# Split-GELU gate, fp32: loads on ScalarE's queue, stores on SyncE's, GELU in place, redundant waits dropped

## Chip, cores, metric

One core of one Trainium2 chip. The metric is the device time of one execution in microseconds (us). The kernel before took 470.53 us (median of 3 runs, 470.52 to 470.63). "Faster" or "slower" here start at 2%.

## The reference

```python
def setup_inputs():
    batch, seq, dim = (32, 512, 2048)
    return {'x': np.random.randn(batch, seq, dim).astype(np.float32)}

def reference(x):
    half_dim = x.shape[-1] // 2
    x1, x2 = x[..., :half_dim], x[..., half_dim:]
    gelu_x1 = 0.5 * x1 * (1 + erf(x1 / np.sqrt(2)))
    return (gelu_x1 * x2).astype(np.float32)
```

134.22 MB are read, 67.11 MB written, and per output element there is one GELU and one multiply.

## The kernel before

16 tiles of 128 partitions x 8 rows x 2048 columns; two x tiles and two o tiles. A load is 8.39 MB, a store 4.19 MB. The first and the last tile are cut into pieces.

```python
R = 8
xpool = tile_pool(name="xpool", bufs=2)
opool = tile_pool(name="opool", bufs=1)
o_tiles = [opool.tile([P, R, half], ...) for k in range(2)]

def load(i):
    x_tile = xpool.tile([P, R, dim], ...)
    for rows in (slice(0, 4), slice(4, 8)) if i == 0 else (slice(0, 8),):
        dma = nc.sync.dma_start(out=x_tile[:, rows, :], in_=x_t[i][:, rows, :])
        before_gelu[i % 2].append(dma.ins)
    return x_tile
# ... store(queue, i, o_tile, rows): the same for a store
ahead = [load(0), load(1)]
for i in range(n_tiles):
    # ... steps: row ranges of a tile, (0,5),(5,8) in the middle tiles
    for lo, hi in steps:
        nc.scalar.activation(out=o_tile[:, rows, :], in_=x_tile[:, rows, :half], func=GELU)
        mul = nc.vector.tensor_mul(out=o_tile[:, rows, :], in0=o_tile[:, rows, :],
                                   in1=x_tile[:, rows, half:])
        for ins in before_gelu[i % 2]:
            tc.declare_no_dep(mul.ins, ins, reason="ScalarE waited for it")
        # ... pieces: store on nc.sync if last, else on nc.scalar
    if not pieces:
        store(nc.sync if i == n_tiles - 2 else nc.scalar, i, o_tile, slice(0, R))
    if i + 2 < n_tiles:
        ahead.append(load(i + 2))
```

GELU writes into the o tile, so it has to wait for the store that still reads that o tile.

Of the kernel before, what the change touches and what calls it, by code (L numbers as in the profile page):

```python
# [1 line left out]

# [4 lines left out]

GELU = mybir.ActivationFunctionType.Gelu


@with_exitstack
def kernel(
    ctx: ExitStack,
    tc: tile.TileContext,
    x: bass.AP,
    out: bass.AP,
):











    nc = tc.nc
    P = nc.NUM_PARTITIONS  # L30

    x_flat = x.flatten_outer_dims()
    out_flat = out.flatten_outer_dims()
    n_rows, dim = x_flat.shape
    half = dim // 2

    R = 8
    x_t = x_flat.rearrange("(n p r) d -> n p r d", p=P, r=R)
    o_t = out_flat.rearrange("(n p r) d -> n p r d", p=P, r=R)
    n_tiles = x_t.shape[0]  # L40

    xpool = ctx.enter_context(tc.tile_pool(name="xpool", bufs=2))
    opool = ctx.enter_context(tc.tile_pool(name="opool", bufs=1))
    o_tiles = [opool.tile([P, R, half], out.dtype, name=f"o{k}_tile") for k in range(2)]

    def load(i):
        x_tile = xpool.tile([P, R, dim], x.dtype, name="x_tile")
        for rows in (slice(0, 4), slice(4, 8)) if i == 0 else (slice(0, 8),):
            dma = nc.sync.dma_start(out=x_tile[:, rows, :], in_=x_t[i][:, rows, :])  # L49
            before_gelu[i % 2].append(dma.ins)  # L50
        return x_tile

    def store(queue, i, o_tile, rows):
        dma = queue.dma_start(out=o_t[i][:, rows, :], in_=o_tile[:, rows, :])
        before_gelu[i % 2].append(dma.ins)


    before_gelu = [], []

    ahead = [load(0), load(1)]  # L60
    for i in range(n_tiles):
        x_tile = ahead.pop(0)
        o_tile = o_tiles[i % 2]
        last = i == n_tiles - 1
        pieces = i == 0 or last
        steps = ((0, 2), (2, 4), (4, 8)) if pieces else ((0, 5), (5, 8))
        muls = []
        for lo, hi in steps:
            rows = slice(lo, hi)
            tc.keep_in_program_order(  # L70
                nc.scalar.activation(  # L71
                    out=o_tile[:, rows, :], in_=x_tile[:, rows, :half], func=GELU
                )
            )
            mul = nc.vector.tensor_mul(  # L75
                out=o_tile[:, rows, :],
                in0=o_tile[:, rows, :],
                in1=x_tile[:, rows, half:],
            )
            for ins in before_gelu[i % 2]:  # L80
                tc.declare_no_dep(mul.ins, ins, reason="ScalarE waited for it")
            muls.append(mul.ins)
            if pieces and hi % 4 == 0:
                store(nc.sync if last else nc.scalar, i, o_tile, slice(hi - 4, hi))
        before_gelu[i % 2].extend(muls)
        if not pieces:
            store(nc.sync if i == n_tiles - 2 else nc.scalar, i, o_tile, slice(0, R))
        if i + 2 < n_tiles:
            ahead.append(load(i + 2))


# [1 line left out]
_INS = ['x']  # L93
_OUTS = [((32, 512, 1024), 'float32')]


# [23 lines left out]
```

## Time and profile before

A queue here is the list of DMAs that one engine issues. A DMA lands when the engines that wait for it see that all its bytes have arrived. The DMA share is the mean busy share of the core's 16 DMA engines.

| | before |
|---|---|
| time, median | 470.53 us |
| span of the profile (first to last instruction of the program) | 469.1 us |
| VectorE, ScalarE busy | 30%, 25% |
| DMA share, 1.7 to 467.9 us | 1.00 |
| bytes over the span | 429 GB/s |

The prediction below shows the lines that carry this. Two more views are needed. The first is the groups of instructions of the kernel before, different shapes apart (line, engine, operation, output<-inputs, shapes, count | busy us, mean ns of one | idle before, and what ended it; DVE is VectorE, ACT ScalarE, SP SyncE, and a q behind a name marks DMA issues):

```profile
L75 DVE TENSOR_TENSOR o_tile<-o_tile,x_tile 128x5120 f32<-128x5120 f32 x14 | 76.9, 5492 | 279.9 <-ACT o_tile L71 279.9
L71 ACT ACTIVATE o_tile<-x_tile 128x5120 f32<-128x5120 f32 x14 | 62.6, 4469 | 301.2 <-DMA out_dram<-o_tile 280.3 <-DMA x_tile<-in_x_dram 20.9
```

The last column shows ScalarE waiting for stores (`out_dram<-o_tile`) in nearly all its idle time. The second is the start of the timeline:

```profile
0.72 1.28 ACT L71 ACT_TABLE_LOAD   x1 [0.72 <-PEq L104]
0.73 403.84 SPq L49 DMA_DIRECT2D x_tile<-in_x_dram  x17
```

ScalarE loads its activation table while SyncE issues the first load.

### The profile page before, as it was taken

The numbers are of one execution on the slowest core, as the hardware profiler recorded it, in microseconds if no ns is written. First come the engines' busy times: TensorE is split into PE (matmuls) and PEld (weight loads), VectorE is DVE, ScalarE is ACT, GpSimd is POOL, SyncE is SP. The second block draws the span as 40 slices with busy tenths as digits, with TensorE's granted clock in tenths as the row PEclk, the third lists the DMA queues.
The fourth block names the chain that finished last, engine by engine and source line by source line (L and its number), as shares of the span: only waits on it lengthen the run. The fifth ranks groups of instructions, "written<-read, shape, count | busy, mean of one in ns | idle before, by whom it ended". The sixth has DMA issues, their size and how long they took to land.

```text
span 469.1 us, 179 instructions
## 1 busy us (share of the span) xinstructions
DVE 140.5 (30%) x34; ACT 115.5 (25%) x35; POOL 0.2 (0%) x4
## 2 busy tenths in 40 slices
DVE  0330615206051160611506015070250702407042
ACT  1320606041060410605005050050601406014060
POOL 0000000000000000000000000000000000000000
DMA  8999999999999999999999999999999999999998
GB/s 358 447 447 447 414 391 492 402 402 447 492 402 402 447 469 425 402 441 408 492 402 425 425 492 402 402 447 486 408 402 444 455 441 402 441 408 486 408 406 355
DMA packets 5041, 201.34 MB, mean 429 GB/s; under 512 B 560, under 2 KB 560, under 8 KB 560
## 3 DMA queue, kind: packets, MB, share of 16 engines
q1 hardware_dynamic: 2880, 142.61, 70.4%
q10 hardware_dynamic: 2160, 58.72, 29.0%
q14 instruction: 1, 0.01, 0.0%
HBM read 134.22 MB, written 67.11 MB: 429 GB/s over the span
## 4 chain that ended last, share of the span: by engine, by line
DMA 75%; DVE 14%; ACT 8%; ACTq 0%; issue 0%; SPq 0%
DMA out_dram<-o_tile 66%; DVE o_tile L75 14%; DMA x_tile<-in_x_dram 10%; ACT o_tile L71 8%; ACTq L115 0%; SPq L49 0%
## 5 line engine op out<-in xcount | busy, mean ns | idle before, releaser
L75 DVE TENSOR_TENSOR o_tile<-o_tile,x_tile 128x5120 f32<-128x5120 f32 (+3 forms) x34 | 140.5, 4171 | 320.4 <-ACT o_tile L71 320.4
L71 ACT ACTIVATE o_tile<-x_tile 128x5120 f32<-128x5120 f32 (+3 forms) x34 | 114.3, 3407 | 340.1 <-DMA out_dram<-o_tile 302.4
L71 ACT ACT_TABLE_LOAD x1 | 1.3, 1283 | 0.7 <-PEq L104 0.7
L104 POOL MEMSET const-bfloat16-1.0<- 128x1 bf16 x1 | 0.1, 101 | 0.0
L104 POOL MEMSET const-uint8-127<- 128x1 uint8 x1 | 0.1, 101 | 0.0
L104 POOL MEMSET const-float32-0.0<- 128x1 f32 x1 | 0.1, 98 | 0.2 <-issue 0.2
L104 POOL MEMSET const-float32-1.0<- 128x1 f32 x1 | 0.1, 98 | 0.0
## 6 DMA issues: line engine op xcount, KB each, us to landing
out_dram<-o_tile ACTq DMA_DIRECT2D x13, 4096.0 KB, 44.8
x_tile<-in_x_dram SPq DMA_DIRECT2D x2, 4096.0 KB, 16.8
out_dram<-o_tile ACTq DMA_DIRECT2D x2, 2048.0 KB, 34.3
out_dram<-o_tile SPq DMA_DIRECT2D x1, 4096.0 KB, 25.2
out_dram<-o_tile SPq DMA_DIRECT2D x2, 2048.0 KB, 7.5
x_tile<-in_x_dram SPq DMA_DIRECT2D x15, 44.6
```

The lines of the kernel that those rows point to most:

```text
L71: nc.scalar.activation(out=o_tile[:, rows, :], in_=x_tile[:, rows, :half], func=GELU)
L75: mul = nc.vector.tensor_mul(out=o_tile[:, rows, :], in0=o_tile[:, rows, :], in1=x_tile[:, rows, half:],)
L104: nc = _bacc.Bacc("TRN2", target_bir_lowering=False, num_devices=1)
```

## The change

The intent: each queue gets one direction; ScalarE no longer waits for a store before GELU (it writes x's own half); waits that another wait implies are declared away. `x_users` and `o_users` list the earlier instructions on the same x and o tile.

```diff
-    xpool = ctx.enter_context(tc.tile_pool(name="xpool", bufs=2))
+    xpool = ctx.enter_context(tc.tile_pool(name="xpool", bufs=1))
+    x_tiles = [xpool.tile([P, R, dim], x.dtype, name=f"x{k}_tile") for k in range(2)]
+    def no_wait(ins, others):
+        for other in others:
+            tc.declare_no_dep(ins, other, reason="implied by another wait")
...
-            dma = nc.sync.dma_start(out=x_tile[:, rows, :], in_=x_t[i][:, rows, :])
+            dma = nc.scalar.dma_start(out=x_tile[:, rows, :], in_=x_t[i][:, rows, :])
...
                 nc.scalar.activation(
-                    out=o_tile[:, rows, :], in_=x_tile[:, rows, :half], func=GELU
+                    out=x_tile[:, rows, :half], in_=x_tile[:, rows, :half], func=GELU
                 )
...
+            no_wait(gelu.ins, x_users[i % 2])
...
             mul = nc.vector.tensor_mul(
                 out=o_tile[:, rows, :],
-                in0=o_tile[:, rows, :],
+                in0=x_tile[:, rows, :half],
                 in1=x_tile[:, rows, half:],
             )
-            for ins in before_gelu[i % 2]:
-                tc.declare_no_dep(mul.ins, ins, reason="ScalarE waited for it")
+            no_wait(mul.ins, loads[i] + x_users[i % 2] + o_users[i % 2])
...
-            store(nc.sync if i == n_tiles - 2 else nc.scalar, i, o_tile, slice(0, R))
+            nc.sync.dma_start(out=o_t[i], in_=o_tile)
...
```

More of the change, by code (lines that the diff above doesn't have):

```diff
@@ L40 @@
     n_tiles = x_t.shape[0]
-    xpool = ctx.enter_context(tc.tile_pool(name="xpool", bufs=2))
+    xpool = ctx.enter_context(tc.tile_pool(name="xpool", bufs=1))
     opool = ctx.enter_context(tc.tile_pool(name="opool", bufs=1))
+    x_tiles = [xpool.tile([P, R, dim], x.dtype, name=f"x{k}_tile") for k in range(2)]
     o_tiles = [opool.tile([P, R, half], out.dtype, name=f"o{k}_tile") for k in range(2)]
+    def no_wait(ins, others):
+        for other in others:
+            tc.declare_no_dep(ins, other, reason="implied by another wait")
+    x_users, o_users = ([], []), ([], [])
+    loads = {}
     def load(i):
-        x_tile = xpool.tile([P, R, dim], x.dtype, name="x_tile")
+        x_tile = x_tiles[i % 2]
+        loads[i] = []
         for rows in (slice(0, 4), slice(4, 8)) if i == 0 else (slice(0, 8),):
-            dma = nc.sync.dma_start(out=x_tile[:, rows, :], in_=x_t[i][:, rows, :])
-            before_gelu[i % 2].append(dma.ins)
-        return x_tile
-    def store(queue, i, o_tile, rows):
-        dma = queue.dma_start(out=o_t[i][:, rows, :], in_=o_tile[:, rows, :])
-        before_gelu[i % 2].append(dma.ins)
-    before_gelu = [], []
-    ahead = [load(0), load(1)]
+            dma = nc.scalar.dma_start(out=x_tile[:, rows, :], in_=x_t[i][:, rows, :])
+            loads[i].append(dma.ins)
+    load(0)
+    load(1)
     for i in range(n_tiles):
-        x_tile = ahead.pop(0)
-        o_tile = o_tiles[i % 2]
+        x_tile, o_tile = x_tiles[i % 2], o_tiles[i % 2]
         last = i == n_tiles - 1
@@ L66 @@
         steps = ((0, 2), (2, 4), (4, 8)) if pieces else ((0, 5), (5, 8))
-        muls = []
+        gelus, muls = [], []
         for lo, hi in steps:
             rows = slice(lo, hi)
-            tc.keep_in_program_order(
+            gelu = tc.keep_in_program_order(
                 nc.scalar.activation(
-                    out=o_tile[:, rows, :], in_=x_tile[:, rows, :half], func=GELU
+                    out=x_tile[:, rows, :half], in_=x_tile[:, rows, :half], func=GELU
                 )
             )
+            no_wait(gelu.ins, x_users[i % 2])
             mul = nc.vector.tensor_mul(
                 out=o_tile[:, rows, :],
-                in0=o_tile[:, rows, :],
+                in0=x_tile[:, rows, :half],
                 in1=x_tile[:, rows, half:],
             )
-            for ins in before_gelu[i % 2]:
-                tc.declare_no_dep(mul.ins, ins, reason="ScalarE waited for it")
+            no_wait(mul.ins, loads[i] + x_users[i % 2] + o_users[i % 2])
+            gelus.append(gelu.ins)
             muls.append(mul.ins)
             if pieces and hi % 4 == 0:
-                store(nc.sync if last else nc.scalar, i, o_tile, slice(hi - 4, hi))
-        before_gelu[i % 2].extend(muls)
+                part = slice(hi - 4, hi)
+                nc.sync.dma_start(out=o_t[i][:, part, :], in_=o_tile[:, part, :])
         if not pieces:
-            store(nc.sync if i == n_tiles - 2 else nc.scalar, i, o_tile, slice(0, R))
+            nc.sync.dma_start(out=o_t[i], in_=o_tile)
+        x_users[i % 2].extend(gelus + muls + loads[i])
+        o_users[i % 2].extend(muls)
         if i + 2 < n_tiles:
-            ahead.append(load(i + 2))
+            load(i + 2)
 _INS = ['x']
```

## The prediction

> **What bounds the kernel now.** I read the page's busy shares first, then its DMA lines, then the busy time by stretch, and only then the waits.
>
> ```profile
> DVE 140.5 (30%) x34; ACT 115.5 (25%) x35; POOL 0.2 (0%) x4
> ...
> DMA  8999999999999999999999999999999999999998
> ...
> q1 hardware_dynamic: 2880, 142.61, 70.4%
> q10 hardware_dynamic: 2160, 58.72, 29.0%
> ...
> HBM read 134.22 MB, written 67.11 MB: 429 GB/s over the span
> ```
>
> VectorE and ScalarE are idle for 70% and 75% of the span. The 16 DMA engines show 90% or more in every slice but the first and the last, and their two queues' packets add up to 70.4 + 29.0 = 99.4% of the span. Both queues move bytes equally fast: 70.4% of 16 x 469.1 us is 5284 us for 142.61 MB, so 27.0 GB/s per engine; 29.0% is 2177 us for 58.72 MB, also 27.0 GB/s. So neither the queue nor the direction matters to the rate; bytes do.
>
> Where is the missing 0.6%? The stretches say it (columns: stretch, its length, busy time of VectorE, ScalarE and GpSimd, clock, DMA share, GB/s).
>
> ```profile
> 0.00:1.70 1.70, 0.00 (x0) 0.98 (x1) 0.20 (x4) 1.00 0.00 0
> 1.70:467.90 466.20, 140.48 (x34) 114.56 (x35) 0.00 (x0) 1.00 1.00 432
> ```
>
> From 1.70 to 467.90 us the DMA share is 1.00. The span has 1.7 us before the first packet (start barrier, then a load issued at 0.73 us, whose packets follow about 1.0 us later) and 1.2 us after the last one (landing of the store, the closing barrier). The floor of this program is therefore 201.33 MB at 432 GB/s = 466.0 us, plus 1.7, plus 1.2: 468.9 us, against a span of 469.1. The kernel stands within 0.1% of what its bytes allow.
>
> The waits look as if they contradict this:
>
> ```profile
> DVE o_tile L75 <- ACT o_tile L71: 320.4, 18, 20.9
> ACT o_tile L71 <- DMA out_dram<-o_tile: 302.4, 14, 22.0
> ACT o_tile L71 <- DMA x_tile<-in_x_dram: 37.8, 3, 20.9
> ```
>
> ScalarE waits 302.4 us for stores, which is just the wait that the change removes. But these are idle times of engines that do not set the end. What one tile in the middle does, and how long its transfers take to land:
>
> ```profile
> 100.48 7.12 ACT L71 ACTIVATE o_tile<-x_tile 128x5120 f32<-128x5120 f32 x2 [21.78 <-DMA out_dram<-o_tile]
> 104.98 8.76 DVE L75 TENSOR_TENSOR o_tile<-o_tile,x_tile 128x5120 f32<-128x5120 f32 x2 [20.14 <-ACT o_tile L71]
> 113.77 0.36 ACTq L54 DMA_DIRECT2D out_dram<-o_tile  x1
> ...
> out_dram<-o_tile ACTq DMA_DIRECT2D x1, 4096.0 KB, 44.7
> x_tile<-in_x_dram SPq DMA_DIRECT2D x1, 44.5
> ```
>
> The last two lines are the store and the load issued at 113.77 us: the load lands at 158.3 us, the store at 158.5. GELU starts at 158.49, on the later of the two.
>
> **What the Trainium skill says.** "DMA: Bandwidth & Descriptors", section "Issuing engines are not separate DMA queues": transfers from SyncE and ScalarE run on the same 16 DMA engines and interleave; using several issuers saves only issue time. This trace agrees: equal rates on both queues, worked out above. The same page, "Where 436 GB/s comes from", puts the ceiling of the path at 435 GB/s; the 432 here, over the whole stretch, leaves nothing to win in rate. "ScalarE: Activation LUTs", "What ACT_TABLE_LOAD costs", gives about 1283 ns for the load of the activation table and 186 ns + 0.833 ns per element for an ACTIVATE without pointer operands: 4451 ns for 5120 elements. The trace has 1.28 us and 4469 ns. "VectorE: DVE Perf Modes", the tier table, has fp32 tensor_tensor of 2048 elements at 2293 ns; the trace has 2288. The formula has no term for where the output lies, so in-place GELU should cost the same.
>
> **The change, part by part.**
>
> Queues swapped. No bytes, shapes or counts change: 17 loads and 18 stores before and after. A load issue takes 0.33 us on SyncE and a store issue 0.36 us on ScalarE; these sit inside the 15 us of slack worked out below, except the first. ScalarE passes the start barrier at the same moment as SyncE (its table load starts at 0.72 us, SyncE's first issue at 0.73). Here is a choice: does ScalarE load its table before or after it issues loads? A table load belongs to the first GELU, and the code issues loads 0 and 1 before it, so I expect it after the three issues, at about 2 us, long before GELU needs it at 12.9 us. Cost then 0.0. If it comes first, the first load issues 1.28 us later and the whole run ends 1.3 us later, since the DMA is never idle afterwards. I give that 20%.
>
> In the loop the new load stands in ScalarE's order behind the two GELUs of its tile and waits for VectorE's last multiply of that tile, so it is issued where it is now (113.77 us). ScalarE's next work is the GELU of the next tile, whose load lands some 15 us later, so this blocks nothing. SyncE now holds only stores, in order. The 2:1 ratio of bytes per load and per store is unchanged, and both queues stay filled.
>
> GELU in place. It writes x's own half and no longer waits for the store of two tiles ago; the multiply takes over that wait. Now GELU may start when the load lands, 0.2 us (158.3 against 158.5) before the store. The multiply starts at the later of (load landing + 4.48 us of first GELU) and the store's landing: 4.3 us after the store, not 4.5. The gain is 0.2 us of latency per tile, and that lies in slack: when the pair lands at about 100.4 us, the next load and store (8.39 + 4.19 MB, issued at 84.87 us) are still wholly outstanding, 29.0 us of DMA work at 434 GB/s, while the next issues come 13.3 us later. The reserve is 15.7 us per tile; making it 15.9 buys nothing.
>
> Dropped waits. Each is at most a 17 ns semaphore instruction of an idle sequencer; 0.0 us.
>
> The end. Load 15 lands at 448.8 us and the last compute starts at 449.17. The store issued at 433.30 lands 25.2 us later, 458.5, and covers the DMA until then. The first half of the last tile is stored from 455.6, the second from 460.9; the first is 2.10 MB, so it keeps the DMA busy until about 463, while the second's packets are ready about 1 us after its issue, 461.9. There is about 1 us to spare, and the change starts this chain up to 0.4 us earlier. Nothing won, nothing lost. Sum: 0.0 us, and 0.2 x 1.3 = 0.3 us on average for the table load.
>
> **The rivals.**
>
> The removed wait was real, and a faster chain pays: the chain of waits on the page goes through stores, GELU and multiply, with 7.8% for GELU and 14% for the multiply; if all first-GELU waits vanished, 14 x 4.5 = 63 us. Against it: the DMA share of 1.00 from 1.70 to 467.90 us. No chain can end before its bytes have moved, so the best case is 468.9 of span, about 0.2 us better.
>
> Loads on ScalarE's queue are held up behind a GELU. If a load were ordered after the next tile's GELU, it would be issued when that tile's load has landed plus 7.1 us of GELU and 1 us to the first packet; meanwhile only 4.19 MB of store (9.7 us) is outstanding. Even that barely fits; with another few us of delay there would be gaps of 1 to 3 us on each of 14 tiles, 480 to 510 us. For it: ScalarE is in order and now carries both. Against it: today's stores stand at the very same place of ScalarE's order and leave within 30 ns of the multiply's end.
>
> The table load goes first: +1.3 us, as above.
>
> **Range and chances.** The mean of the cases is 470.53 + 0.3, of which I keep little because it is one chance in five: 470.6 us. Downward there is only 0.2 us of span plus scatter (the three runs spread 0.1 us[...]). Upward there is 1.3 us. So 469.8 to 472.0 us eight times in ten. Faster by 2% would need 461.1 us, below the 466.0 us of the bytes alone: 0.5%. Slower by 2% needs 9.4 us of idle DMA, which only the second rival gives: 1.5%.
>
> **What would show it right or wrong.** Right: DMA slices stay at 9 throughout, the bytes change sides (about 134 MB on the queue that ScalarE feeds, 67 on SyncE's), ScalarE's waits name the loads and no store, the ACTIVATE and TENSOR_TENSOR durations stay at 4469 and 5492 ns, and VectorE still mostly waits for ScalarE. The table load's place is seen in the first row of ScalarE. Wrong: DMA shares below 1.00 in the middle, loads that issue well after the multiply's end, a multiply slowed by its strided first operand, or loads and stores on swapped queues that no longer land together, so that the last store begins later.

## The result, and the profile after

471.46 us median (471.11 to 471.99, 6 runs) against 470.53 us (470.46 to 470.73, 6 runs). The ratio is 1.002, 95% interval 1.0007 to 1.0033. Ratios here are the mean time of one kernel's fast runs over that of the other's of the same rounds, so not quite the ratio of the medians. So: the same within 2%, and slower by 0.2% beyond noise.

From the page of the changed kernel, the DMA slices and the queues (packets, MB, share of 16 engines' span):

```profile
DMA  8999999999999999999999999999999999999998
...
q10 hardware_dynamic: 2448, 134.22, 66.3%
q1 hardware_dynamic: 2592, 67.11, 33.2%
```

The bytes have changed sides as intended, 134 MB and 67 MB, and the DMA is as full as before. By stretch (columns as in the prediction):

```profile
0.00:1.70 1.70, 0.00 (x0) 0.00 (x0) 0.20 (x4) 1.00 0.00 0
1.70:467.90 466.20, 140.48 (x34) 115.54 (x35) 0.00 (x0) 1.00 1.00 432
```

The same 1.00 and 432 GB/s; the only difference is ScalarE's 0.98 us in the first 1.7 us, which is the table load that has moved. The waits of the changed kernel (who <- for whom: us in total, times, longest):

```profile
ACT x_tile L72 <- DMA x_tile<-in_x_dram: 338.4, 17, 21.9
DVE o_tile L77 <- ACT x_tile L72: 320.0, 18, 21.4
```

The 302.4 us for stores are gone from ScalarE, and it waits 338.4 us for loads: 302.4 + 37.8 = 340.2 before. A wait changed its name and kept its length. One tile in the middle, from the timeline:

```profile
100.79 7.12 ACT L72 ACTIVATE x_tile<-x_tile 128x5120 f32<-128x5120 f32 x2 [21.88 <-DMA x_tile<-in_x_dram]
105.29 8.76 DVE L77 TENSOR_TENSOR o_tile<-x_tile 128x5120 f32<-128x5120 f32 x2 [20.25 <-ACT x_tile L72]
114.08 0.36 ACTq L58 DMA_DIRECT2D x_tile<-in_x_dram  x1
```

The load leaves ScalarE 0.03 us after the multiply's end (105.29 + 8.76 = 114.05), so sharing an engine with GELU delays nothing. The groups, shapes apart:

```profile
L77 DVE TENSOR_TENSOR o_tile<-x_tile 128x5120 f32<-128x5120 f32 x14 | 76.9, 5492 | 279.7 <-ACT x_tile L72 279.7
L72 ACT ACTIVATE x_tile<-x_tile 128x5120 f32<-128x5120 f32 x14 | 62.6, 4469 | 301.0 <-DMA x_tile<-in_x_dram 301.0
```

5492 and 4469 ns, to the nanosecond those of before: GELU in place and a multiply with a strided first operand cost the same. The start of ScalarE's timeline, and the last stores, which SyncE issues:

```profile
0.74 1.35 ACTq L58 DMA_DIRECT2D x_tile<-in_x_dram  x3
2.11 1.28 ACT L72 ACT_TABLE_LOAD   x1 [2.11 <-issue]
...
455.31 5.57 SPq L87 DMA_DIRECT2D out_dram<-o_tile  x2
```

The three loads are issued first (0.74 us against 0.73), the table follows. The last tile's stores go out at 455.31 us and 5.2 us later, 0.3 us earlier than before, and it helps nothing.

Both profiles have a span of 469.1 us. The 0.9 us must then be outside the span, or in the scatter between runs: each run of the changed kernel has its own span, 468.7 to 469.6, and time minus span (the time of a run less its own span) is 2.29 to 2.41 us in all six. In the profiled run of before it was 470.87 - 469.1 = 1.8. That became the open question of the experiments, next to the claim that the compute chain has a reserve.

### The profile page after: what moved, and what is told of

The parts are those of the page before. It is cut to its first block, busy times and chain, and to the rows that moved or that the text cites. A ratio compares the mean times of both kernels' runs of the same rounds, so it can differ in the third digit from the quotient of the medians.

```text
span 469.1 us, 178 instructions
## 1 busy us (share of the span) xinstructions
DVE 140.5 (30%) x34; ACT 115.5 (25%) x35; POOL 0.2 (0%) x4
## 4 chain that ended last, share of the span: by engine, by line
DMA 75%; DVE 14%; ACT 8%; ACTq 1%; issue 0%
DMA x_tile<-in_x_dram 75%; DVE o_tile L77 14%; ACT x_tile L72 8%; ACTq L119 0%; ACTq L58 0%
## 5 line engine op out<-in xcount | busy, mean ns | idle before, releaser
L77 DVE TENSOR_TENSOR o_tile<-x_tile 128x5120 f32<-128x5120 f32 (+3 forms) x34 | 140.5, 4171 | 320.0 <-ACT x_tile L72 320.0
L72 ACT ACTIVATE x_tile<-x_tile 128x5120 f32<-128x5120 f32 (+3 forms) x34 | 114.3, 3407 | 338.4 <-DMA x_tile<-in_x_dram 338.4
```

The source lines that it names most:

```text
L72: nc.scalar.activation(out=x_tile[:, rows, :half], in_=x_tile[:, rows, :half], func=GELU)
L77: mul = nc.vector.tensor_mul(out=o_tile[:, rows, :], in0=x_tile[:, rows, :half], in1=x_tile[:, rows, half:],)
```

## The experiments

Twelve kernels, in three calls, each call on one chip with runs of the kernel before. "Before" took 470.63, 470.63 and 470.56 us (medians).

**1. The changed kernel again.** No edit.

> The changed kernel once more, to see whether its 0.9 us (ratio 1.002) repeat. Both profiles so far have a span of 469.1 us and the same DMA busy time, so the 0.9 us should again lie outside the span: time minus span 2.3 to 2.4 us. If they are scatter of one chip, the ratio is 1.000 here.

Measured: 471.31 us (471.03 to 471.58, 5 runs), before 470.63; ratio 1.0013 (1.0001 to 1.0026). Mean span 468.92 against 468.88 of before; mean time minus span 2.35 against 1.78. So of the 0.62 us between the mean times, 0.57 lie outside the span and 0.04 in it. The difference repeats and is not in the part where the kernel's work is.

**2. Queues only.** Before, with

```diff
-            dma = nc.sync.dma_start(out=x_tile[:, rows, :], in_=x_t[i][:, rows, :])
+            dma = nc.scalar.dma_start(out=x_tile[:, rows, :], in_=x_t[i][:, rows, :])
...
-                store(nc.sync if last else nc.scalar, i, o_tile, slice(hi - 4, hi))
+                store(nc.sync, i, o_tile, slice(hi - 4, hi))
...
-            store(nc.sync if i == n_tiles - 2 else nc.scalar, i, o_tile, slice(0, R))
+            store(nc.sync, i, o_tile, slice(0, R))
```

> Only the queues swapped, GELU still into o_tile with its old waits. If the swap of queues costs the 0.9 us (ScalarE's queue for loads), the ratio is 1.002. If the extra time is an instruction fetch after the end that depends on how many instructions each engine has, VectorE has as few here as before, and the ratio should be 1.000. In either theory the DMA share from 1.7 to 467.9 us stays 1.00 and the span 469.1.

Measured: 470.62 us, ratio 1.000 (0.9988 to 1.0013); span 468.88, time minus span 1.78. The swap of queues is worth nothing and costs nothing.

**3. In place and dropped waits only.** The changed kernel, with

```diff
-            dma = nc.scalar.dma_start(out=x_tile[:, rows, :], in_=x_t[i][:, rows, :])
+            dma = nc.sync.dma_start(out=x_tile[:, rows, :], in_=x_t[i][:, rows, :])
...
-                nc.sync.dma_start(out=o_t[i][:, part, :], in_=o_tile[:, part, :])
+                (nc.sync if last else nc.scalar).dma_start(out=o_t[i][:, part, :], in_=o_tile[:, part, :])
-            nc.sync.dma_start(out=o_t[i], in_=o_tile)
+            (nc.sync if i == n_tiles - 2 else nc.scalar).dma_start(out=o_t[i], in_=o_tile)
```

> GELU in place and the waits dropped, queues as before. If the dropped waits and in-place GELU were worth anything, it would show here undisturbed: the prediction says 0.0 us, ratio 1.000 (the rival of a shorter chain: 0.87 at its best). If the new waits of VectorE lengthen the end by an instruction fetch, ratio 1.002; if the swap of queues does it, 1.000.

Measured: 471.07 us, ratio 1.0011 (0.9999 to 1.0024); mean span 469.14, time minus span 2.04. The freed wait of ScalarE brings nothing here either. Outside the span there is half of the extra time, between the two theories as I had put them: neither named 2.04.

**4. Redundant waits left in.** The changed kernel, with

```diff
-        for other in others:
-            tc.declare_no_dep(ins, other, reason="implied by another wait")
+        return
```

> The changed kernel with every redundant wait left in (VectorE then waits for up to four semaphores per multiply). Prediction: the dropped waits are worth 0.0 us, so within 0.3 us of the changed kernel. If waits cost the DMA anything, the span grows over 469.1; if only the number of instructions per engine matters to the fetch at the end, the span stays and time minus span differs from the changed kernel's 2.4.

Measured: 470.94 us, ratio 1.0006 (0.9993 to 1.002); span 469.08, time minus span 1.86. The kernel with 30 more wait instructions on VectorE is not slower than the changed one (470.94 against 471.31): the dropped waits are worth 0.0 us in the span, and outside it their absence goes with a longer time.

**5. to 7. Padding the instruction streams.** Tiny instructions at the start, where the engine idles anyway: 14 GELUs on ScalarE of the changed kernel; 30 multiplies on its VectorE; 14 multiplies on VectorE of the kernel before. Shown for 5; 6 and 7 have their own count, take the multiply and put the tile in `opool`.

```diff
     load(1)
+    pad = xpool.tile([P, 4], x.dtype, name="pad")
+    nc.gpsimd.memset(pad, 0.0)
+    for _ in range(14):
+        nc.scalar.activation(out=pad, in_=pad, func=GELU)   # or: nc.vector.tensor_mul(out=pad, in0=pad, in1=pad)
```

> The changed kernel with 14 tiny GELUs (128x4) on ScalarE at the start, where it waits 9 us for the first load anyway, and one small memset on GpSimd. ScalarE then has 74 instructions instead of 60 (the queues-only kernel had 74 and its time minus span was 1.78 us). If the 0.6 us outside the span hangs on how many instructions the engines' streams hold, time minus span moves away from 2.35, most likely to 1.8, the span stays 468.9 to 469.2, and the kernel is as fast as before (ratio 1.000). If it comes from the change itself (queues with in-place GELU), it stays at 2.35, ratio 1.0013.

> The changed kernel with 30 tiny multiplies (128x4) on VectorE at the start: 86 instructions instead of 56, as many as the kernel with all waits kept, whose time minus span was 1.86 us. Stream length theory: time minus span about 1.9, span unchanged at 469.0, ratio about 1.0006. If it was the waits themselves that shortened that kernel's time, time minus span stays 2.35.

> The kernel before with 14 tiny multiplies on VectorE at the start: 56 instructions as in the changed kernel, with nothing else changed. Stream length theory: time minus span leaves 1.78 us, up to some 0.6 us, with the span unchanged at 468.9; that would make the kernel before slower by 0.1% with no part of the change in it. If the time outside the span belongs to the change, it stays 1.78 and the ratio 1.000.

Measured: 471.13 us (ratio 1.001, 0.9998 to 1.0023), 471.02 us (1.0009, 0.9996 to 1.0021) and 470.90 us (1.0007, 0.9993 to 1.002). The ratios alone say little. Span and time minus span say more, since the latter scatters by only some 0.05 us around its mean within a kernel (most in experiment 1: 2.22 to 2.41). Instructions are counted in the built programs; the kernels 9 to 12 are described below and stand here because they test the same thing:

| kernel | instructions ScalarE, VectorE | mean span | mean time minus span |
|---|---|---|---|
| before (call 1, call 2) | 72, 42 | 468.88, 468.87 | 1.78, 1.77 |
| queues only (2) | 74, 42 | 468.88 | 1.78 |
| before + 14 multiplies (7) | 72, 56 | 468.90 | 2.03 |
| in place only (3) | 69, 56 | 469.14 | 2.04 |
| changed + 14 GELUs (5) | 74, 56 | 469.06 | 2.06 |
| changed + 1 GELU (8, below) | 61, 56 | 469.20 | 2.05 |
| changed (1) | 60, 56 | 468.92 | 2.35 |
| changed + 30 multiplies (6) | 60, 86 | 469.16 | 1.89 |
| changed, waits kept (4) | 60, 86 | 469.08 | 1.86 |
| before (call 3) | 72, 42 | 468.80 | 1.79 |
| hardly any compute (9) | 39, 44 | 469.75 | 1.77 |
| multiplies twice (10) | 73, 84 | 469.77 | 1.76 |
| multiplies three times (11) | 73, 112 | 508.02 | 1.77 |
| late loads (12) | 61, 56 | 475.55 | 2.05 |

Experiment 7 is the clean one: nothing of the change is in it, the span does not move (468.90), and the time outside grows by 0.26 us. With 42 or 44 instructions on VectorE it is 1.77 to 1.79, with 56 it is 2.03 to 2.06, with 84 or more again 1.76 to 1.89. With 56 on VectorE, ScalarE at 60 goes with a further 0.3 us (2.35), at 61 or more it does not. So the time outside the span goes with the lengths of the instruction streams (the instructions of one engine, in order), up and down, and not with a queue, a wait or in-place GELU as such. The padded kernels also carry one memset on GpSimd and one instruction more on SyncE; experiment 12 has neither, and at 61 and 56 it too has 2.05. Of the three numbers that I had expected for 5 to 7, only that of 6 was met (1.89 for 1.9); 5 gave 2.06 and not 1.8, 7 gave part of its "up to 0.6". Why a certain length costs 0.3 us is open: the trace records nothing of the engines after the span. A fetch of instructions was my guess. The traces of the changed kernel have a packet of the instruction queue at 471.2 to 471.3 us, after the span, where the kernel before has one at 453.7 us. But experiments 8 and 12 also have one after the span, with only 2.05 us, and experiment 7 has its own at 453.6 us with 2.03, so the place of that packet doesn't explain it.

**8. Activation table before the loads.** The changed kernel, with the order of ScalarE's issues fixed and

```diff
+    warm = opool.tile([P, 4], x.dtype, name="warm")
+    nc.gpsimd.memset(warm, 0.0)
+    nc.scalar.activation(out=warm, in_=warm, func=GELU)
     load(0)
```

> The changed kernel with one tiny GELU ahead of the loads on ScalarE, so that the activation table is loaded before the first load is issued. The prediction's branch: the first load issues 1.28 us later plus about 0.2 us for the tiny GELU, the DMA is busy ever after, so the span grows by 1.3 to 1.5 us, to about 470.4. If some slack in the rest takes it up, the span stays 469.0.

Measured: 471.13 us, ratio 1.0013 (1.0000 to 1.0026); mean span 469.20. The expected 1.3 us do not come. The timeline shows why:

```profile
0.73 1.28 ACT L65 ACT_TABLE_LOAD   x1 [0.73 <-PEq L113]
0.87 1.34 ACTq L59 DMA_DIRECT2D x_tile<-in_x_dram  x3
2.02 0.21 ACT L65 ACTIVATE warm<-warm 128x4 f32<-128x4 f32 x1
```

The loads stand behind the table load and the tiny GELU in ScalarE's order, yet the first is issued at 0.87 us, while the table is still loading and before the GELU has run. ScalarE's sequencer (the part that reads its instructions and issues its DMAs) hands work to the engine and goes on to the next DMA. The issue comes 0.05 us after the end of GpSimd's memset (0.82 us), for which the tiny GELU waits; that this wait held it is likely, not shown. The first issue is 0.13 us later (0.87 against 0.74), and that may be the memset's doing.

**9. Hardly any compute.** The changed kernel, its loads and stores kept, GELU gone and the multiply cut to 128x4 elements per tile. Its output is wrong, which doesn't matter for the time.

```diff
+    for o_tile in o_tiles:
+        nc.vector.memset(o_tile, 0.0)
...
-                nc.scalar.activation(...)
...
             mul = nc.vector.tensor_mul(
-                out=o_tile[:, rows, :],
-                in0=x_tile[:, rows, :half],
-                in1=x_tile[:, rows, half:],
+                out=o_tile[:, lo, :4],
+                in0=x_tile[:, lo, :4],
+                in1=x_tile[:, lo, half : half + 4],
             )
...
```

> The same loads and stores on the same queues, with the compute of a tile (13.3 us from landing to issue) cut down to one 128x4 multiply, about 0.1 us. The result is wrong on purpose[...]. DMA-bound theory: the span stays at 468.7 to 469.1 us although 98% of the compute is gone. Rival (the chain of load or store, GELU and multiply sets the pace): 14 tiles would save up to 13 us each, 290 us at the least and certainly more than 2%.

Measured: 471.01 us (470.87 to 471.06, and one run of 473.18), before 470.56; ratio 1.002 (0.9998 to 1.0041), which takes in the run of 473.18. From its page:

```profile
span 469.3 us, 145 instructions
...
DVE  6500000000000000000000000000000000000000
...
DMA  8999999999999999999999999999999999999998
```

VectorE does next to nothing after the two memsets (6.9 us each; then 18 multiplies of 0.16 us), ScalarE computes nothing, and the span is that of the full kernel. From 1.70 to 467.90 us the rate is still 432 GB/s. The bytes alone take 469 us. Every theory in which GELU, multiply or the waits between them set the pace falls here.

**10. and 11. Using up the reserve.** The changed kernel with the multiply of each middle tile repeated once, or twice:

```diff
+        for lo, hi in () if pieces else steps * 1:      # 11: steps * 2
+            rows = slice(lo, hi)
+            mul = nc.vector.tensor_mul(
+                out=o_tile[:, rows, :],
+                in0=x_tile[:, rows, :half],
+                in1=x_tile[:, rows, half:],
+            )
+            no_wait(mul.ins, loads[i] + x_users[i % 2] + o_users[i % 2])
+            muls.append(mul.ins)
```

> The changed kernel with every middle tile's multiply done twice: 8.76 us more of VectorE per tile, 14 tiles. The prediction put the reserve at 15.7 us between the landing of a pair and the moment the DMA would run dry; about 1 us of that goes to the way from issue to first packet. So 8.76 us fit: span 468.9 to 469.2, DMA share 1.00. If VectorE's chain counted, 14 x 8.76 = 123 us.

> The multiply of every middle tile done three times: 17.5 us more per tile. Then a pair is issued 13.3 + 17.5 = 30.8 us after a landing, its first packets come 1 us later, and the pair in flight lasts 29.0 us: the DMA runs dry for 2.8 us. The pair issued late lands late by the same amount, so the next one is in time, and a gap should come at every second tile: 7 x 2.8 = 20 us, time about 490 (485 to 500). If the reserve is larger than worked out, it stays at 471; if every tile has its gap, 510.

Measured, once: 471.52 us, ratio 1.002 (1.0005 to 1.0035), mean span 469.77, time minus span 1.76. The span is 0.85 us above that of experiment 1, more than expected, but 123 us of multiplies cost no more than that. Its middle by stretch:

```profile
72.00:449.00 377.00, 226.59 (x52) 92.25 (x26) 0.00 (x0) 1.00 1.00 432
```

VectorE is busy for 226.59 of 377 us and the DMA share is still 1.00.

Measured, twice: 509.74 us, ratio 1.0833 (1.0817 to 1.0849). By stretch, and the two GELUs of neighbouring tiles from the timeline:

```profile
110.00:487.00 377.00, 313.20 (x72) 85.22 (x24) 0.00 (x0) 1.00 0.97 399
140.00:143.00 3.00, 0.34 (x1) 2.18 (x1) 0.00 (x0) 1.00 0.65 175
```

```profile
203.65 7.12 ACT L72 ACTIVATE x_tile<-x_tile 128x5120 f32<-128x5120 f32 x2 [24.11 <-DMA x_tile<-in_x_dram]
...
235.24 7.12 ACT L72 ACTIVATE x_tile<-x_tile 128x5120 f32<-128x5120 f32 x2 [24.47 <-DMA x_tile<-in_x_dram]
```

The reserve is used up: the DMA share falls to 0.97, with a dip in which it is 0.65 for 3 us, about 1 us of idle DMA, and a tile takes 31.6 us here where it took 29.0. Now the chain does set the pace. The size is not the 20 us expected but 39. I had the loop right (landing, 30.7 us of compute, issue, transfer, for two tiles in turn), but had its gaps at every second tile, where the trace has one at every tile, and took a transfer for 29.0 + 1.0 us from issue to landing; the page has

```profile
x_tile<-in_x_dram ACTq DMA_DIRECT2D x15, 32.1
```

32.1 us. Half of 30.7 + 32.1 is 31.4 us per tile, 2.4 more than 29.0. From the landing of load 3 at 109.7 us to that of load 15 at 487.0 us the trace has 12 tiles, so 29 us. The rest is the first full tile: only the second half of store 0 and load 2 (10.5 MB) are in flight beside it, and load 3 lands 9 us later than in experiment 1. Seen from the DMA, the 39 us are two halves. Each engine idles 20 us more, 7.7 of them at one stretch from 70.8 us on. And the packets' own time grew by 19, from 466.5 to 485.5 us per engine: after each dry spell the first 32 KB packet of an engine takes 1.94 us and its first 64 KB packet 3.15, where the others take 1.21 and 2.42. That the idle half equals the 20 us expected is chance.

**12. Loads behind the next tile's GELU.** The changed kernel, the order of ScalarE's issues fixed, and

```diff
-        if i + 2 < n_tiles:
-            load(i + 2)
+        if 1 <= i < n_tiles - 1:
+            load(i + 1)
```

> The prediction's second rival made real: on ScalarE every load stands behind the GELUs of the next tile, so it is issued when that tile's load has landed plus 7.1 us. The prediction said that the 9.7 us of a store still outstanding then would barely cover this (471 to 480). On second thoughts I expect worse: the store shares the DMA with the load ahead of it and is mostly drained when the load lands; worked through with the store taking a third of the packets, some 3 us of it are left, so about 5 us of idle DMA per tile, 14 tiles: 540 us (520 to 560).

Measured: 476.43 us (476.12 to 476.65, and one run of 481.43); ratio 1.0159 (1.0103 to 1.0214), so unclear at 2%. The prediction's text was nearer than my second thoughts, but neither had the reason. From the timeline and by stretch:

```profile
168.21 8.76 DVE L79 TENSOR_TENSOR o_tile<-x_tile 128x5120 f32<-128x5120 f32 x2 [21.49 <-ACT x_tile L74]
...
191.91 4.47 ACT L74 ACTIVATE x_tile<-x_tile 128x5120 f32<-128x5120 f32 x1 [21.07 <-DMA x_tile<-in_x_dram]
191.91 0.34 ACTq L59 DMA_DIRECT2D x_tile<-in_x_dram  x1
```

```profile
60.00:455.00 395.00, 114.16 (x27) 92.60 (x26) 0.00 (x0) 1.00 1.00 431
...
460.00:462.00 2.00, 1.72 (x1) 2.00 (x1) 0.00 (x0) 1.00 0.00 0
```

The load stands behind two GELUs and is issued at the very moment the first of them starts, not 7.1 us later: as in experiment 8, the sequencer doesn't wait for the engine. But it is held by the GELU's semaphore (the signal for which an instruction waits), that is until the previous load's landing: the load's own wait, for the multiply that frees its tile, was over at 176.97 us (168.21 + 8.76). That alone costs 1 us to the first packet, which the store's remainder covers: the DMA share is 1.00 in the middle with a single load in flight. So the rival as the prediction meant it, a load issued 7.1 us late, was not built. Of the 5.1 us of span lost in the profile, 2.8 come at the end: the last load lands at 455.27 us instead of 448.8, and the DMA is idle from 459.8 to 462.6 us before the last tile's stores. Another 2.0 are longer packets (468.5 us per engine against 466.5).

No version beat the kernel before. With the DMA full from 1.7 us to the end, only fewer bytes or a higher rate could make a clearly faster one.

## Why the prediction was right

The time lay within the range (471.46 in 469.8 to 472.0) and within 2%, as forecast at 98%. By its own steps:

- **The DMA bounds the kernel; floor 468.9 us of span.** Right, and shown: without compute the span is still 469.1 to 469.3 us in three of four runs, at the same 432 GB/s (experiment 9). The floor is an estimate: it takes this kernel's own rate, so it shows that there are no gaps and not that the rate is the highest, and spans of 468.7 us were measured.
- **Queues swapped: 0.0.** Shown: ratio 1.000, the spans equal (experiment 2). Loads leave ScalarE within 0.03 us of the multiply's end.
- **GELU in place and dropped waits: 0.0 in the span.** Supported: durations equal within 1 ns, ScalarE's 302 us of store waits turned into load waits, and neither experiment 3 nor 4 gains. Spans there are 0.2 us above that of before, which is also how far spans of one kernel scatter.
- **A reserve of 15.7 us per tile.** Bracketed: 8.76 us fit, 17.5 us do not. Its exact size was not measured. What 17.5 us cost was expected wrongly: the first packets after a dry spell are slower (experiment 11).
- **The end has 1 us to spare.** Consistent: the last stores go out 0.3 us earlier and the span does not change.
- **The table load, 0.3 us on average.** Half wrong. It came after the issues, as thought likelier. But the branch was mis-sized: where it comes first, the first issue is 0.13 us later and not 1.3, because a DMA issue doesn't wait for ScalarE's work in progress (experiment 8). The 0.1 us that I added for it had no ground.
- **What it lacked.** It set the median of 470.53 us beside a span of 469.1 us and took the 1.4 us between them as fixed. They are not fixed, and the span was that of a run of 470.87 us: time minus span is 1.78 before, 2.35 after. That is 0.57 of the 0.62 us lost in experiment 1. In the first comparison it is 0.57 of the 0.93 us between the means; the other 0.36 would lie in the span, where runs of the changed kernel scatter from 468.7 to 469.6, and this part stays open. That the range held the loss was luck: its upper part stood for the table load, which did not cost anything.

The rival of a shorter chain (63 us of waits removed) falls by experiment 9. The rival of loads held up behind GELU falls in its mechanism by experiment 12: what delays a load is not a GELU at work ahead of it but a GELU that still waits.

## What to carry to other kernels

Before removing a wait, ask of the DMA share in the middle of the run whether anything can be gained: at 1.00 over 466 us, ScalarE's largest wait (302 us) was worth nothing, and it came back under another name. Size the reserve from the bytes in flight at a landing against the compute until the next issue, and test it by adding work rather than by removing waits. Where two kernels differ by a few tenths of a us, compare span and time minus span apart before looking for a cause in the kernel.

## What the Trainium skill lacked or had wrong

- "Runtime: NRT & Kernel Launch", "The launch sequence", lists costs around a kernel, "depending on engine count and DMA setup", but not that they vary with the instruction streams; "Instruction fetch mechanics" calls the cost of crossing from one block of instructions to the next mostly hidden. The time outside the span went from 1.78 to 2.35 us with the lengths of the instruction streams, and 14 tiny multiplies in the kernel before cost 0.26 us there with the span unchanged (experiment 7). The mechanism is open.
- "ScalarE: Activation LUTs", "What ACT_TABLE_LOAD costs", gives the 1.28 us but not that a DMA issue that follows passes it: issued at 0.87 us during a table load from 0.73 to 2.01 us. "Perfetto Trace Analysis", "Sequencer Loop", which says that engine instructions are pushed into a queue, agrees with this. But it has them wait for their semaphores after that push, and in experiment 12 a GELU that waited held the load behind it from 176.97 us, when the load's own wait was over, to 191.91 us, when the GELU started.
- "DMA: Bandwidth & Descriptors" has figures for the first byte and the fixed cost of a DMA, but nothing on slower packets after a dry spell: in experiment 11 an engine's first 32 KB packet took 1.94 us against 1.21 and its first 64 KB packet 3.15 against 2.42, and 12.58 MB took 32.1 us from issue to landing, against 29.0 us for the same bytes at full rate plus 1.0 us to the first packet. In the section that the prediction cites for 435 GB/s, "Where 436 GB/s comes from", a note says that between HBM and on-chip memory the HBM side binds, at about 358 GB/s; this one core moved 432 GB/s for 466 us.
